# Pooling data loaded into two operand tiles of the input projection, within the projection's last block

## The chip, the cores and the metric

One core of a Trainium2 chip runs the whole program. The metric is the device time in microseconds of one execution. Matrix products run on TensorE (PE); VectorE (DVE), ScalarE (ACT) and GpSimd (POOL) do elementwise work; DMA transfers are issued from the queues of SyncE (SP) and ACT.

## The reference

One decoder block on 1024 tokens of width 1024, in float32: half a SwiGLU FFN, a mixer, half a second SwiGLU FFN, and a final norm. The mixer has one input projection and two branches, attention and pooling, which are merged by gates:

```python
u = rms_norm(h, mix_norm[l])
proj = u @ w_in[l]
q = proj[..., o:o + ATTN_WIDTH]...      # and k, v
pz = proj[..., o:o + POOL_WIDTH]
gates = jax.nn.sigmoid(proj[..., o:o + N_BRANCHES * D_MODEL].reshape(B, S, N_BRANCHES, D_MODEL))
y_attn = dilated_mixture_attention(q, k, v) @ w_branch_attn[l]
y_pool = multiscale_pool(pz, pool_w[l], pool_scale[l]) @ w_branch_pool[l]
merged = gates[:, :, 0] * y_attn + gates[:, :, 1] * y_pool
h = h + merged @ w_out[l]
```

`multiscale_pool` takes, in four groups of 128 channels, trailing means over 2, 4, 8 and 16 tokens minus the token, and multiplies each group by its own 128 x 128 matrix. Its result, 512 channels for each token, is what the change is about.

## The kernel before

Float32 accuracy is had by splitting each operand into a rounded part and a rest (`hi` and `lo`) and taking three products (`three`, L119): hi with hi, hi with lo, lo with hi.

**The input projection** (L1292 on) works in 19 blocks (`MIX`, L110): nine for queries, keys and values, two for the pooling input, eight for the gates; the last is gate block 7. A block is multiplied in seven products instead of eight, in the order 1, 6, 2, 7, 5, 4, 3 (`ORDER`, L317), each of twelve matmuls (`Sevens.product`, L309). Each product has its own left operand made of the normed input, a pair of tiles hi and lo of 128 x 4 x 512 floats (1 MB each) that stays in SBUF for the whole projection: product 1 reads `b11`, 2 reads `b21`, 3 `b22`, and 4 to 7 read `t4`, `t1`, `t2`, `t3` (L363). In traces, where digits are left out of names, `xhi_b_mix` is any of the three b tiles, `xhi_t_mix` any of the four t tiles. So the last block reads `b11` for the last time in its first product, `b21` in its third, `b22` in its seventh.

The loop over k (L1297) runs over all products of all blocks. At a given k it also issues the transfers of that place in the order: results of a finished block go to DRAM (`gate` L1007, `late_w` L1130, `pool` L1093 with `pool_dram` g for pooling group g), and the attention's first data are brought in: `first_ring` at k = n - 12, `load_values(0)` and `load_branch(0)` at k = n - 4, with n the number of products.

**The attention** (L1714 on) works in rounds q, each on two tiles of queries. TensorE does in a round: the scores (L1479), the transposes `tp` of the round before (L1526), up to eight matmuls `yp` of the pooling branch (`branch`, L1604 to L1620), and the values `o` of the round before that (L1559). ACT does the exponents (L1506) that the transposes need. The matmuls `yp` fill the waiting time of TensorE: for each output block d they take weights `wab` and, in the order k = 2, 3, 0, 1, the four pooling groups `y_pool[k]`, three matmuls for each group.

Queries and keys of the next 8 tiles come as a ring: eight loads `qk_in` (L1143, L1144), four for the queries and four for the keys, from `load_ring`; then ACT (L1152) and POOL (L1153) split them in place, `split_ring` n = 0, 1 for the first four loads in one round and n = 2, 3 for the other four in the next. In rounds 0 to 3 the kernel works on ring 0 and splits the second pair (ring 1) in rounds 2 and 3.

**Order.** Both stretches are under `tc.manual_schedule()`: the instructions of each engine stand in the order in which the code is written, and each queue issues its transfers in that order, one waiting for the next. Semaphores are put in by the framework; it gives each transfer one of eight in turn, and a transfer waits until the one that had its semaphore before has landed. SBUF places are handed on tile by tile: a tile in a place that was used before waits for the last reader of the tile that lay there (`reuse_waits="tile"`, L160).

**The four pooling tiles** lie in pools of their own, opened behind the projection (L1337) in the place where `b21` and `b11` lay. Their loads (L1602, named `pool_in<-pool`) are the first of the attention's transfers:

```python
    y_pool = [left_b.enter_context(sbuf(f"pool{g}")).tile([P, 2, S], F32R, name=f"pool_in{g}") for g in range(4)]
...
        for g in (2, 3, 0, 1):
            load_pool(g)
        load_ring(uses[1], ring_tile)
        load_branch(1)
```

Of the kernel before, what the change touches and what calls it, by code (L numbers as in the profile page):

```python
# [10 lines left out]
F32 = mybir.dt.float32  # L11
F32R = mybir.dt.float32r
# [4 lines left out]
P = 128  # L17
S = 1024
# [108 lines left out]
def tile_block(  # L127
# [28 lines left out]
    nc = tc.nc  # L156
    ve, ac, gp, pe = nc.vector, nc.scalar, nc.gpsimd, nc.tensor

    def sbuf(name, side="left", bufs=1):
        return tc.tile_pool(name=name, bufs=bufs, side=side, reuse_waits="tile")  # L160
# [13 lines left out]
    def row(name):  # L174
        return keep.tile([P, 1024], F32, tag="raw", bufs=RAW_BUFS, name=name)
# [109 lines left out]
    def sums_of_x(pool, name, order, **kw):  # L285
        return {
            s: tuple(pool.tile([P, 4, HALF], F32R, name=f"x{part}_{s}_{name}", **kw) for part in ("hi", "lo"))
            for s in order
        }
# [329 lines left out]
    def spilled(name):  # L619
        return [  # L620
            [dram.tile([P, js.stop - js.start, HALF], F32, name=f"gs_{name}{m}_{js.start}") for js in PAIRS]
            for m in range(7)
        ]
# [268 lines left out]
        return pairs  # L892

    sums = spilled("f1")
    mstack, dstack = ExitStack(), ExitStack()
    X_mix = {}

    def down_room(name):
        return dstack.enter_context(sbuf(f"down_{name}"))

    def room1():
        scope.close()
        X_mix.update(sums_of_x(mstack.enter_context(sbuf("xa")), "mix", ("b21", "b11")))
        return down_room("f1")

    def load_residual():
# [25 lines left out]
    pool_dram = [dram.tile([P, 2, S], F32, name=f"pool{g}") for g in range(4)]  # L932
# [164 lines left out]
    def load_pool_w():  # L1097
        pool_w_in.append(fm.tile([P, 2, HALF], F32R, tag="y", bufs=2, name="pool_w"))
        nc.sync.dma_start(pool_w_in[0].bitcast(F32), late_w[0])
# [3 lines left out]
    def load_table(g):  # L1103
        tables[g] = keep.tile([P, 2, HALF], F32, tag="gain", bufs=1, name=f"table{g}_in")
        nc.sync.dma_start(tables[g], table_dram[g])
# [30 lines left out]
    def load_ring(u, tile):  # L1136

        ring[u] = []
        for a in range(2):
            y, hi = tile(F32, f"qk{u}_{a}_in"), tile(F32R, f"qk{u}_{a}_hi")  # L1140
            for n in range(2):
                r = n * HD + 16
                nc.sync.dma_start(y[r:r + 48], qk_dram[u][a, n, 16:])  # L1143
                nc.sync.dma_start(y[r - 16:r].rearrange("r (t c) -> r t c", t=2),  # L1144
                                  rot_dram[u][1][:, a, n].rearrange("t r c -> r t c"))
            ring[u].append((hi, y.bitcast(F32R), y))

    def split_ring(u, n):

        hi, lo, y = ring[u][n // 2]  # L1150
        c = (LOWS, HIGHS)[n % 2]
        ac.activation(hi[:, c], y[:, c], AF.Copy)  # L1152
        gp.tensor_tensor(lo[:, c], y[:, c], hi[:, c].bitcast(F32), op=OP.subtract)  # L1153

    def first_ring():
        load_ring(0, lambda dt, n: keep.tile([P, S], dt, tag="h", bufs=NT, name=n))
        yield 4
        for n in range(4):
            split_ring(0, n)
            yield 1  # L1160
# [4 lines left out]
    def row_part(name):  # L1165
        return keep.tile([P, S], F32R, tag="raw", bufs=RAW_BUFS, name=name)
# [6 lines left out]
            nc.sync.dma_start(v.bitcast(F32), v_dram[u][:, part])  # L1173


    pool_in = {}

    def load_branch(d):
        w, gb = row_part(f"wab{d}"), row(f"gb{d}")
        nc.sync.dma_start(w.rearrange("p (q c) -> p q c", q=2).bitcast(F32), late_w[1 + d][:, :, 256:768])  # L1180
        nc.sync.dma_start(gb, gate_dram[d][:, 1])
        pool_in[d] = (w.rearrange("p (q c) -> p q c", q=2), gb)
# [5 lines left out]
    items = [(q, m) for q in range(len(MIX)) for m in ORDER if q >= AHEAD or m not in (1, 2)]  # L1188
# [103 lines left out]
    with tc.manual_schedule():  # L1292
        entry.run(high_mix, after_mix)

        later, results = [], {}
        load_table(0)
        for k in range(len(items) + 4):  # L1297
            if k - 1 in results and items[k - 1][1] == 1:
                mixes[items[k - 1][0]].out(1, results.pop(k - 1))
            mix_operand(k + 2)  # L1300
            if k - 2 in range(len(items)):
                mixes[items[k - 2][0]].activate()
            if k < len(items):
                q, m = items[k]
                results[k] = mixes[q].quad.run(m)
                if m == 7 and 0 < q <= len(LATE):
                    later.append([k + 1, split_late(q - 1)])
            if k - 1 in results:
                q, m = items[k - 1]
                mixes[q].out(m, results.pop(k - 1))  # L1310
                if m == 3:
                    later.append([k, mixes[q].finish()])
            for job in list(later):
                if job[0] <= k:
                    wait = next(job[1], 0)
                    job[0] = k + wait
                    if not wait:
                        later.remove(job)
            if k == 7 * 6:
                load_pool_w()  # L1320
            if k == 7 * 12:
                tables.clear()
                mask = keep.tile([P, 384], F32, tag="gain", bufs=1, name="mask")
                nc.sync.dma_start(mask, c_mask)
            if k == len(items) - 12:
                later.append([k, first_ring()])
            if k == len(items) - 4:
                load_values(0, row_part)
                load_branch(0)
    assert not later  # L1330
    mstack.close()
    mix_stack.close()
# [1 line left out]


    left_b = ExitStack()
    y_pool = [left_b.enter_context(sbuf(f"pool{g}")).tile([P, 2, S], F32R, name=f"pool_in{g}") for g in range(4)]  # L1337
    sums_o = left_b.enter_context(sbuf("sums_o"))
    ep = left_b.enter_context(sbuf("weights"))
    a2 = left_b.enter_context(sbuf("a2", bufs=2))  # L1340
# [257 lines left out]
    by_pool = [dram.tile([P, S], F32, name=f"by_pool{d}") for d in range(KT)]  # L1598
    stores = []

    def load_pool(g):
        nc.sync.dma_start(y_pool[g].bitcast(F32), pool_dram[g])  # L1602

    def branch(n):  # L1604

        d, half = divmod(n, 2)
# [105 lines left out]

    first = first_w_o()
    with tc.manual_schedule():  # L1714
        for g in (2, 3, 0, 1):
            load_pool(g)
        load_ring(uses[1], ring_tile)
        load_branch(1)
        factors = [make_factors(hp, eng) for hp, eng in enumerate((gp, ve))]
        combines = [[combine(hp, half, adds, lower) for half in range(2)]  # L1720
                    for hp, (adds, lower) in enumerate((((gp, gp), gp), ((gp, ve), ve)))]
        splits = {}
        for q in range(N // 2):
            send()
            scores(2 * q)
            scores(2 * q + 1)
            if q > 0:
                trans_p(q - 1)
                splits[q - 1] = split_p(q - 1)
                next(fill, None)  # L1730
                if q % 4 != 3:
                    next(fill, None)
            if q > 1:
                values(q - 2)
            if q > 2:
                gather(2 * q - 6)
                gather(2 * q - 5)
            masked(2 * q)
            masked(2 * q + 1)
            u, i = divmod(q, NT // 2)  # L1740
            if 0 < u < len(uses) - 1 and i == 0:
                load_ring(uses[u + 1], ring_tile)
            if q > 0:
                advance(splits[q - 1], 2)
            if i > 1 and u + 1 < len(uses):
                split_ring(uses[u + 1], 2 * i - 4)
                split_ring(uses[u + 1], 2 * i - 3)
            end_branches()
            exponents(2 * q)
            exponents(2 * q + 1)  # L1750
            house(2 * q)
            house(2 * q + 1)
        send()
        right_b.close()
        load_ya(3)
        load_merge(0)
        load_merge(1)
        open_w_o()
        q = N // 2
        trans_p(q - 1)  # L1760
        splits[q - 1] = split_p(q - 1)
        advance(factors[1])
        next(fill, None)
        values(q - 2)
        gather(2 * q - 6)
        gather(2 * q - 5)
        advance(splits[q - 1], 2)
        advance(factors[1], 2)
        next(fill, None)
        end_branches()  # L1770
        values(q - 1)
        for s in range(2 * q - 4, 2 * q):
            gather(s)
        for n in range(8):
            advance(combines[1][n // 4])
            if n != 3:
                next(fill, None)
            end_branches()
            send()
            if n == 3:  # L1780
                load_merge(2)
        for k in (3, 4):
            load_merge(k)
    assert next(fill, None) is None
    left_b.close()


    x2, m1 = ExitStack(), ExitStack()
# [342 lines left out]
```

## Time and profile before

| | |
|---|---|
| time, median of 3 runs | 1957.8 us (1957.8 to 1959.87) |
| profiled execution | span 1955.6 us, from its first to its last instruction; no other time of it is given |
| mean granted TensorE clock | 0.994 |
| input projection's last block and the attention's first rounds | about 1038 to 1083 us of the span |
| `pool_in<-pool` | 4 loads of 1024 KB, issued 1052.7 to 1056.6 us |

In the rows of a timeline the first number is the start in us, the second the time taken, then engine, line, operation, output <- inputs, shapes, and how many instructions the row merges; a bracket gives the idle time of the engine before it and what ended it. SPq and ACTq are the DMA queues of those engines; there the time is that of the issue, and the landing comes later. In a row of groups the numbers behind the bar are busy us, mean ns of one, and idle time before with what ended most of it. In a row of waits they are us in total, times, and the longest.

### The profile page before, as it was taken

To read this page: it belongs to the slowest core of one execution; us is meant where nothing else is said; L and a number is where in the kernel's file an instruction comes from. 1 tells how busy PE (TensorE), PEld (TensorE's weight loads), DVE (VectorE), ACT (ScalarE), POOL (GpSimd) and SP (SyncE) were. 2 spreads that over 40 slices of the span, in tenths; PEclk is the share of its full clock that TensorE was granted. 3 is DMA by queue.
4 is the path that set the end of the run, shared out by engine and by line. 5 is a ranking of instruction groups with operands and counts; after the bars stand their busy time and mean duration, and the time that the engine had idled before them with its cause. 6 is when DMAs were issued, how large, how long until landed. Compare 5 with 4: busy or idle time off the path is not lost. (4 is left out here: it accounts for less than half of the span.)

```text
span 1955.6 us, 25018 instructions
## 1 busy us (share of the span) xinstructions
PE 1914.1 (98%) x8938; PEld 1579.7 (81%) x8938; DVE 1343.5 (69%) x2012; ACT 759.4 (39%) x1361; POOL 741.1 (38%) x557
## 2 busy tenths in 40 slices
PE   9999999999999999999998999999999999999997
PEld 7788888888888887888876878887788888878885
DVE  7776556557686876568774886887665556577766
ACT  6333333334344533334344662253333333333343
POOL 5333333332222444445454365543333333322231
PEclk9999999999999999999998999999999999999999
DMA  4155223336465546765658887643523223454653
GB/s 185 44 194 169 85 86 117 121 124 208 156 246 201 167 120 230 232 220 185 232 218 289 241 241 261 253 161 96 190 102 135 82 87 120 139 204 135 212 195 142
DMA packets 147005, 333.57 MB, mean 171 GB/s; under 512 B 20160, under 2 KB 40896, under 8 KB 145344
## 3 DMA queue, kind: packets, MB, share of 16 engines
q1 hardware_dynamic: 138096, 308.00, 45.9%
q10 hardware_dynamic: 8784, 23.96, 3.5%
q8 instruction: 71, 1.16, 0.2%
q14 instruction: 54, 0.44, 0.1%
HBM read 229.61 MB, written 102.30 MB: 170 GB/s over the span
## 5 line engine op out<-in xcount | busy, mean ns | idle before, releaser
L706 PE MATMUL d_f<-bhi_f,alo_f 128*128 128x512 f32 x616 | 240.8, 391 | 2.4 <-POOL alo_f L668 2.2
L706 PE MATMUL d_f<-bhi_f,ahi_f 128*128 128x512 f32 x616 | 240.9, 391 | 0.2 <-ACT ahi_f L664 0.2
L706 PE MATMUL d_f<-blo_f,ahi_f 128*128 128x512 f32 x616 | 240.0, 390 | 0.0
L668 POOL TENSOR_TENSOR alo_f<-g_f,ahi_f 128x512 fp32r<-128x512 f32 x70 | 99.2, 1434 | 298.5 <-ACT ahi_f L664 289.8
L314 PE MATMUL u_mixm<-xhi_t_mix,wc_mixm 128*128 128x512 f32 x608 | 196.0, 393 | 2.7 <-POOL wc_mixm L306 2.3
L314 PE MATMUL u_mixm<-xhi_b_mix,wc_mixm 128*128 128x512 f32 x456 | 149.3, 393 | 2.0 <-DVE y_m L982 2.0
L706 PEld LDWEIGHTS d_f<-bhi_f,alo_f 128*128 128x128 f32 x616 | 115.7, 188 | 29.0 <-POOL alo_f L668 4.0
L314 PEld LDWEIGHTS u_mixm<-xhi_t_mix,wc_mixm 128*128 128x128 f32 x608 | 113.8, 188 | 29.0 <-POOL wc_mixm L306 4.9
L706 PEld LDWEIGHTS d_f<-bhi_f,ahi_f 128*128 128x128 f32 x616 | 115.8, 188 | 24.1 <-ACT ahi_f L664 0.6
L706 PEld LDWEIGHTS d_f<-blo_f,ahi_f 128*128 128x128 f32 x616 | 115.8, 188 | 23.8
L314 PE MATMUL u_mixm<-xlo_t_mix,wc_mixm 128*128 128x512 f32 x304 | 118.6, 390 | 0.0
L306 POOL TENSOR_TENSOR wc_mixm<-s_mixm,wc_mixm 128x512 fp32r<-128x512 f32 x52 | 75.8, 1459 | 99.7 <-ACT wc_mixm L303 84.0
L314 PEld LDWEIGHTS u_mixm<-xhi_b_mix,wc_mixm 128*128 128x128 f32 x456 | 85.7, 188 | 20.7 <-ACT late_hi L1125 2.8
L303 ACT ACTIVATE wc_mixm<-s_mixm 128x512 fp32r<-128x512 f32 x76 | 47.6, 629 | 122.8 <-DVE s_mixm L347 52.1
L314 PE MATMUL u_mixm<-xlo_b_mix,wc_mixm 128*128 128x512 f32 x228 | 88.9, 390 | 0.0
L664 ACT ACTIVATE ahi_f<-g_f 128x1024 fp32r<-128x1024 f32 x84 | 81.8, 974 | 2.0 <-DMA g_f<-gs_f 2.0
L306 POOL TENSOR_TENSOR wc_mixm<-raw,wc_mixm 128x512 fp32r<-128x512 f32 x40 | 60.4, 1515 | 44.9 <-ACT wc_mixm L303 42.0
L664 ACT ACTIVATE bhi_f<-s_f2w 128x512 fp32r<-128x512 f32 x55 | 32.8, 627 | 97.1 <-DVE s_f2w L684 86.8
L1854 PE MATMUL wo<-w_o,o_hi 128*128 128x512 f32 x224 | 69.3, 391 | 0.0
L314 PEld LDWEIGHTS u_mixm<-xlo_t_mix,wc_mixm 128*128 128x128 f32 x304 | 57.2, 188 | 11.7 <-DVE xlo_t_mix L385 0.2
L664 ACT ACTIVATE bhi_f<-s_f1w 128x512 fp32r<-128x512 f32 x55 | 32.9, 630 | 85.1 <-DVE s_f1w L684 80.2
L1616 PE MATMUL yp<-pool_in,wab 128*128 128x512 f32 x192 | 55.7, 426 | 4.2 <-DMA pool_in<-pool 4.2
(1300 smaller groups left out, 5099.8 us busy)
## 6 DMA issues: line engine op xcount, KB each, us to landing
g_f<-gs_f SPq DMA_DIRECT2D x70, 512.0 KB, 4.5
gs_f<-y_f SPq DMA_DIRECT2D x88, 256.0 KB, 2.3
raw<-in_w2a_dram SPq DMA_DIRECT2D x35, 512.0 KB, 4.1
raw<-in_w2b_dram SPq DMA_DIRECT2D x35, 512.0 KB, 4.0
gs_f<-gb_f SPq DMA_DIRECT2D x46, 256.0 KB, 2.3
raw<-in_w1a_dram SPq DMA_DIRECT2D x22, 512.0 KB, 4.6
raw<-in_w3a_dram SPq DMA_DIRECT2D x22, 512.0 KB, 6.3
raw<-in_w1b_dram SPq DMA_DIRECT2D x22, 512.0 KB, 4.5
```

Of the source, the lines that this page charges most:

```text
L303: ac.activation(w[:, 0], src, AF.Copy)
L306: eng.tensor_tensor(w[:, 1], src, w[:, 0].bitcast(F32), op=OP.subtract)
L314: pe.matmul(p, a, b, start=(start and k == 0 and q == 0), stop=(k == 3 and q == 2), skip_group_check=not start)
L664: ac.activation(hi[:, c], src, AF.Copy)
L668: eng.tensor_tensor(lo[:, d], src[:, o], hi[:, d].bitcast(F32), op=OP.subtract)
L706: pe.matmul(self.banks[m][t], l, r, start=(first and q == 0), stop=(last and q == 2))
L1616: pe.matmul(p, a, b, start=(j == 0), stop=(j == 11))
L1854: pe.matmul(banks[m][t], l, r, start=(st == 0 and j == 0 and q == 0), stop=(st == 1 and j == 1 and q == 2))
```

## The change

The tiles of `b11` and `b21` get a stack of pools of their own (`xstack`), which stays open until the attention's end; the other operands are closed with the projection as before. The four pooling tiles have no pools of their own any more: `load_pool` writes pooling group g into one of the four tiles (hi or lo of `b11` or `b21`), seen as 128 x 2 x 1024. Groups 2 and 3 are loaded at k = n - 5, groups 0 and 1 at k = n - 3, inside the projection's loop; the four loads at the head of the attention are gone. In the SP queue of the built program the loads of groups 2 and 3 now stand behind ring 0 and ahead of the last two `late_w` stores, and those of groups 0 and 1 where the first two pooling loads stood before, behind `wab` and `gb` of `load_branch(0)`. The order of all other instructions on every engine stays.

```diff
-    mstack, dstack = ExitStack(), ExitStack()
+    xstack, mstack, dstack = ExitStack(), ExitStack(), ExitStack()
...
-        X_mix.update(sums_of_x(mstack.enter_context(sbuf("xa")), "mix", ("b21", "b11")))
+        X_mix.update(sums_of_x(xstack.enter_context(sbuf("xa")), "mix", ("b21", "b11")))
...
-    pool_in = {}
+    pool_in, y_pool = {}, {}
+
+    def load_pool(g, x, part):
+        y_pool[g] = X_mix[x][part].rearrange("p (q k) c -> p q (k c)", q=2)
+        nc.sync.dma_start(y_pool[g].bitcast(F32), pool_dram[g])
...
+            if k == len(items) - 5:
+                load_pool(2, "b11", 0)
+                load_pool(3, "b11", 1)
             if k == len(items) - 4:
                 load_values(0, row_part)
                 load_branch(0)
+            if k == len(items) - 3:
+                load_pool(0, "b21", 0)
+                load_pool(1, "b21", 1)
...
-    y_pool = [left_b.enter_context(sbuf(f"pool{g}")).tile([P, 2, S], F32R, name=f"pool_in{g}") for g in range(4)]
...
-    def load_pool(g):
-        nc.sync.dma_start(y_pool[g].bitcast(F32), pool_dram[g])
-
...
-        for g in (2, 3, 0, 1):
-            load_pool(g)
         load_ring(uses[1], ring_tile)
...
     left_b.close()
+    xstack.close()
```

## The prediction

> **What bounds the kernel now.** I read the page first, then TensorE's own timeline at the end of the input projection, then the issues of the SP queue there, then the DMA share in short windows.
>
> ```profile
> span 1955.6 us, 25018 instructions
> PE 1914.1 (98%) x8938; PEld 1579.7 (81%) x8938; DVE 1343.5 (69%) x2012; ACT 759.4 (39%) x1361; POOL 741.1 (38%) x557
> L1616 PE MATMUL yp<-pool_in,wab 128*128 128x512 f32 x192 | 55.7, 426 | 4.2 <-DMA pool_in<-pool 4.2
> ```
>
> TensorE is busy for 98% of the span, so what can be won is its idle time and the time in which it runs slowly. The pooling branch `yp` idles 4.2 us, all of it for the four loads of `pool_in` (128 x 2 x 1024 floats, 1.05 MB each). Its mean matmul is 426 ns against 0.39 us for a matmul of the projection (quoted further down), so some of them also ran slowly. Where:
>
> ```profile
> 1056.94 0.33 PE L1479 MATMUL s<-qk_hi,qk_hi 64*128 64x128 f32 x2
> 1061.18 0.71 PE L1526 MATMUL tp<-ident,e 128*128 128x128 f32 x2 [1.39 <-ACT e L1506]
> 1062.74 1.52 PE L1616 MATMUL yp<-pool_in,wab 128*128 128x512 f32 x3
> 1065.63 1.65 PE L1616 MATMUL yp<-pool_in,wab 128*128 128x512 f32 x3 [1.36 <-DMA pool_in<-pool]
> 1069.78 1.22 PE L1616 MATMUL yp<-pool_in,wab 128*128 128x512 f32 x2 [2.50 <-DMA pool_in<-pool]
> 1074.49 1.87 PE L1616 MATMUL yp<-pool_in,wab 128*128 128x512 f32 x7 [0.38 <-DMA pool_in<-pool]
> 1077.36 0.39 PE L1479 MATMUL s<-qk_hi,qk_hi 64*128 64x256 f32 x2
> ...
> 1088.05 0.33 PE L1479 MATMUL s<-qk_hi,qk_hi 64*128 64x128 f32 x2
> 1089.56 2.07 PE L1616 MATMUL yp<-pool_in,wab 128*128 128x512 f32 x8
> 1091.47 0.28 PE L1559 MATMUL o<-ehi,v_in 128*128 128x256 f32 x1
> 1092.99 0.33 PE L1479 MATMUL s<-qk_hi,qk_hi 64*128 64x128 f32 x2
> ```
>
> The loads land one by one: 2 before 1062.74, 3 at 1065.6, 0 at 1069.8, 1 at 1074.5. Undisturbed, eight `yp` take 1091.47 - 1089.56 = 1.91 us and one round (scores, transposes, eight `yp`, values) 1092.99 - 1088.05 = 4.94. From 1062.74 these make 6.85; the kernel needs 14.62 to reach 1077.36. So 7.77 us are lost here, by waits and by the clock:
>
> ```profile
> 1059.53:1062.94 3.41, 1.76 (x12) 0.94 (x9) 1.12 (x7) 3.22 (x10) 0.00 (x0) 0.99 1.01 399
> 1062.94:1073.18 10.24, 6.38 (x25) 3.88 (x24) 2.18 (x9) 2.55 (x9) 0.00 (x0) 0.50 1.02 387
> 1131.21:1134.62 3.41, 3.41 (x11) 2.58 (x10) 3.37 (x13) 3.41 (x12) 2.52 (x2) 0.51 1.04 329
> ```
>
> (Stretch, length, busy us of PE, PEld, DVE, ACT, POOL, granted clock, DMA share, GB/s.) After a stretch of 3.41 us with 1.76 busy the clock is half for 10.24 us, which is three such stretches. At 1131, where TensorE had work all through, one stretch at half clock was all.
>
> **The change part by part.** Nothing is computed differently. In the built program's SP queue two issues move: loads 2 and 3 go from behind `wab` and `gb` to ahead of the last `late_w` stores; loads 0 and 1 stay behind `gb`. The destinations are now the operand tiles b11 and b21 themselves.
>
> ```profile
> 1036.27 0.30 SPq L1144 DMA_DIRECT2D qk_in<-rot  x1
> 1043.44 4.04 SPq L1130 DMA_DIRECT2D late_w<-raw  x2
> 1051.31 0.61 SPq L1180 DMA_DIRECT2D wab<-late_w  x1
> 1052.65 4.22 SPq L1602 DMA_DIRECT2D pool_in<-pool  x4
> 1057.94 0.33 SPq L1143 DMA_DIRECT2D qk_in<-qk  x1
> 1068.46 0.30 SPq L1144 DMA_DIRECT2D qk_in<-rot  x1
> 1072.33 0.30 SPq L1144 DMA_DIRECT2D qk_in<-rot  x1
> ```
>
> *The new wait.* Load 2 must wait for the last block's first product, the last reader of b11. In TensorE's timeline the product behind it, on t2, begins at 1040.53:
>
> ```profile
> 1040.53 0.39 PE L314 MATMUL u_mixm<-xhi_t_mix,wc_mixm 128*128 128x512 f32 x1
> ```
>
> So load 2 can go near 1041. SP has nothing to issue between 1036.6 and 1043.44, so the wait holds up nobody.
>
> *The transfer.* The DMA engines in that time:
>
> ```profile
> 1042.00:1048.00 6.00, 6.00 (x28) 4.97 (x27) 3.36 (x3) 4.32 (x9) 6.00 (x5) 1.00 0.23 91
> 1048.00:1050.00 2.00, 2.00 (x10) 1.67 (x9) 0.69 (x1) 0.40 (x1) 2.00 (x2) 1.00 1.01 401
> ```
>
> At 401 GB/s 2.1 MB take 5.2 us. From about 1042 (a microsecond after issue, my estimate) to 1048 the engines are idle for 0.77 of 6 us, 4.6. So 0.6 us of it pushes back what follows, for from 1048 on the engines are full.
>
> *Whether that hurts.* `wab` had landed at 1057.9, when the ring issue that waits for it went out (1057.94 above); 1058.5 is still ahead of the first `yp` at 1062.74, and 4.8 us of cover were there. Load 0 takes the place of load 2, which landed after 9.3 us at 1062.0: now 1062.6, needed six `yp` into the round, not before 1064. Load 1 takes that of load 3: 1065.6 becomes 1066.2, needed 1062.74 + 1.91 + scores and transposes (1089.56 - 1088.05 = 1.51) + one `yp` = 1066.4. All four waits of `yp` go.
>
> ```profile
> L1602 SPq DMA_DIRECT2D pool_in<-pool x4: 319/376/498, 1052.7 to 1056.6; - x4
> DMA to landing us min/median/max: 9.3/13.4/17.9
> ```
>
> *What stays.* The gap of 1.39 before 1061.18 is ACT's and isn't touched, so the half clock from 1062.94 stays for one stretch, which is then full: half of 3.41, or 1.7, is kept. TensorE's own gain is 7.77 - 1.7 = 6.1.
> The Trainium skill ("TensorE: Matmul & The Clock Gate", section "HAM oscillation — how this bites in real kernels") warns only of idle gaps over some 3.4 us. By it 1.39 would not slow the array and the gain would be 7.8; the row above, where 1.76 busy of 3.41 was enough, speaks against it.
>
> *What is late next.* The attention's second pair of rings (`qk_in`, eight loads in two halves). ACT splits them in its order, ahead of the exponents that TensorE's transposes need:
>
> ```profile
> 1076.52 1.15 ACT L1152 ACTIVATE qk_hi<-qk_in 128x512 fp32r<-128x512 f32 x2 [1.97 <-DMA qk_in<-rot]
> 1080.67 1.14 ACT L1152 ACTIVATE qk_hi<-qk_in 128x512 fp32r<-128x512 f32 x2
> ...
> SPq L1144 <- DMA gate<-y_m: 9.2, 2, 6.2
> L1007 ACTq DMA_DIRECT2D gate<-y_m x2: 326/416/506, 1058.4 to 1058.8; - x2
> DMA to landing us min/median/max: 10.0/11.8/13.5
> ...
> L1144 SPq DMA_DIRECT2D qk_in<-rot x2: 303/303/303, 1072.3 to 1074.5; - x2
> DMA to landing us min/median/max: 3.1/3.8/4.5
> ```
>
> Every DMA of this program takes the next of eight semaphores and first waits for the DMA that had it before; so the rings' issues at 1068.46 and 1072.33 waited for ACT's two gate stores, issued at 1058.4 and 1058.8, landed 10.0 and 13.5 us later. In the changed program the first ring half waits for `v`, `wab` and `gb`, is out by 1060 (`gb` follows `wab` on the queue) and lands some 2 us behind load 1 (as at 1076.5 behind 1074.5): 1068.5, when ACT gets there. The second half still waits for both gate stores, whose issue doesn't move. Bounds for the second store: 1069.5, if it has the engines to itself once SP's queue is dry near 1069, and 1072.3 as now. I take 1071.7, nearer the row, since the first ring half keeps SP's queue full. The last issue follows at 1072.1 and lands 3.1 later (last row above, up to 4.5): 1075.2. ACT then splits at 1075.2 what it splits at 1080.67 now: **5.4 us** earlier, less than TensorE's 6.1. Bounds of that term: 1072.3 + 0.4 + 4.5 = 1077.2, a gain of 3.5; with 1069.5, TensorE's 6.1.
>
> After that every step follows the one before. The third pair of rings starts only some 2.5 us earlier, since it is issued behind the second, but has cover:
>
> ```profile
> L1144 SPq DMA_DIRECT2D qk_in<-rot x1: 303/303/303, 1085.7 to 1085.7; - x1
> DMA to landing us min/median/max: 3.7/3.7/3.7
> ...
> 1095.29 1.15 ACT L1152 ACTIVATE qk_hi<-qk_in 128x512 fp32r<-128x512 f32 x2
> ```
>
> It lands at 1089.4 and is used at 1095.3, so 5.9 us of cover against 5.4 - 2.5 = 2.9 of it used.
>
> *Sum.* Span 1955.6 - 5.4 = 1950.2. The profile shows no time of its own execution beside the span; the median of the runs is 1957.8, so 2.2 us lie around it, and the forecast is 1952.4.
>
> **The rivals.**
> *The rings come in time.* The gate stores land by 1070, and TensorE's own 6.1 us (clock half for one stretch) to 7.8 (for none, where the stretches divide the gap otherwise than in this execution) are won: 1951.7 to 1950.0. For it: fewer loads compete with the store. Against: the store shares the engines until the first ring half has landed.
> *Given back later.* In the attention's middle POOL waits for a load of weights:
>
> ```profile
> POOL w_o_in L1371 <- DMA w_o_in<-in_w_o_dram: 6.9, 1, 6.9
> ```
>
> ACT splits that weight behind POOL and ahead of exponents, so TensorE may stop behind it. If loads there run at the engines' rate, they come earlier only by the 2.5 us of the third rings, so about 3 of 5.4 are lost: gain 2.5, 1955.3. Against: the rows from 1088 to 1093 above show no wait for a load.
> *It doesn't do what it says.* Load 2 gets its place only when b21's reader is done, two products of twelve matmuls later (8 take 1.91 us, so 5.7), at 1046.3: at most the 1.7 us up to 1048 are left to use, and so gained: 1956.1. Against: the two tiles have wait and place of their own.
> *Slower.* Load 2 waits at the head of SP's queue until the whole block is done, when the scores begin at 1056.9, and `late_w`, the gate stores, `v`, `wab` and `gb` stand behind it. With the four pools (4.2 MB), 1.05 for each of the first three and 0.5 for each of the last two these are 8.4 MB, 21 us at 401 GB/s, and 2 for landing: load 1 lands at t + 23 for an issue at t. Against 1074.5 that loses from t = 1051.5 on; at 1056.9 it costs 5.4: 1963.2. Against: b11's reader is the block's first product.
>
> **How the numbers follow.** Chances: forecast 0.50, rings in time 0.20, given back 0.16, not as it says 0.06, slower 0.08. 0.2% (3.9 us) is what a measurement of this kernel tells from no change. Faster by more: the forecast but for its upper end (0.45), the rings in time (0.20) and a part of the third (0.04): 0.69. Slower 0.08, the rest 0.23. The range runs from 1949.5 (7.8 and half a microsecond between runs) to 1956.5, over the third and fourth cases; the forecast's own bounds are 1951.7 to 1954.3.
>
> **What would show it.** Loads 2 and 3 issued near 1041 and landed by 1049; no idle time of `yp` for a load; one stretch at half clock after 1062.9, not three; the scores of 1077.36 near 1071; a wait of ACT's L1152 for `qk_in` of 1 to 2 us near 1075. The forecast is wrong if SP's `late_w` starts after 1044, if `wab` lands after 1062.7, or if TensorE is 5 us ahead at 1085 and not at 1200.

## The result, and the profile after

| | before | changed kernel |
|---|---|---|
| time, median (lowest to highest, runs) | 1958.0 us (1955.9 to 1963.3, 15) | 1954.8 us (1951.4 to 1956.4, 15) |
| ratio of the runs | | 0.9976, 95% interval 0.9969 to 0.9983 |
| profiled execution: time and span | span 1955.6 us | 1953.8 us, span 1951.8 us |

The change makes the kernel faster by 0.24% (0.17 to 0.31), which is 4.7 us (3.3 to 6.1) of 1958; the medians stand 3.2 us apart. 5.4 were forecast, with 3.5 to 6.1 as the bounds of that term.

TensorE's timeline of the changed kernel, from the first scores on. Line numbers behind L1176 are 4 to 9 higher than before in this part, `pool_in` is now called by the tile in which it lies (`xhi_b_mix`, `xlo_b_mix`), and the whole trace runs 0.71 us later from the first scores on (1057.65 for 1056.94). This shift is there before any of the moved loads and is not of the change.

```profile
1057.65 0.33 PE L1488 MATMUL s<-qk_hi,qk_hi 64*128 64x128 f32 x2
...
1061.98 0.71 PE L1535 MATMUL tp<-ident,e 128*128 128x128 f32 x2 [1.47 <-ACT e L1515]
...
1063.68 1.63 PE L1622 MATMUL yp<-xhi_b_mix,wab 128*128 128x512 f32 x3
...
1066.87 0.39 PE L1488 MATMUL s<-qk_hi,qk_hi 64*128 64x256 f32 x2
...
1070.80 0.28 PE L1568 MATMUL o<-ehi,v_in 128*128 128x256 f32 x1
...
1071.95 0.39 PE L1488 MATMUL s<-qk_hi,qk_hi 64*128 64x256 f32 x2
...
1073.49 1.92 PE L1535 MATMUL tp<-ident,e 128*128 128x128 f32 x8 [0.57 <-ACT e L1515]
...
1088.28 0.33 PE L1488 MATMUL s<-qk_hi,qk_hi 64*128 64x128 f32 x2
```

No `yp` waits for a load any more, the scores of 1077.36 come at 1071.95, and those of 1092.99 at 1088.28. Counted from the first scores of the same trace (called t0 from here on), these last ones come at 30.63 us instead of 36.05: 5.42 less. They are the sixth group of scores in the timeline, those of round 6; most expectations below call them "the eighth scores". The expectation of again_after uses the same words for the fourth group: its 25.5 and 20.0 us are 1082.41 - 1056.94 before and 1077.70 - 1057.65 after.

The clock and the DMA engines (stretch, length, busy us of the five engines, granted clock, DMA share, GB/s):

```profile
1059.38:1062.79 3.41, 1.78 (x11) 0.87 (x8) 1.83 (x12) 2.64 (x8) 0.00 (x0) 1.00 0.98 392
1062.79:1066.20 3.41, 3.35 (x10) 2.66 (x11) 1.11 (x2) 2.90 (x12) 0.00 (x0) 0.50 1.03 430
...
1042.70:1048.70 6.00, 6.00 (x28) 4.97 (x27) 3.25 (x3) 4.43 (x9) 6.00 (x5) 1.00 0.96 329
```

One stretch at half clock, where three were. The last row is the time into which loads 2 and 3 went, the same six microseconds that carried 91 GB/s before.

SP's queue, issues only, and the landings of some of them:

```profile
1041.43 0.34 SPq L1180 DMA_DIRECT2D xhi_b_mix<-pool  x1
1041.82 0.43 SPq L1180 DMA_DIRECT2D xlo_b_mix<-pool  x1
1044.14 3.92 SPq L1130 DMA_DIRECT2D late_w<-raw  x2
...
1050.95 0.85 SPq L1184 DMA_DIRECT2D wab<-late_w  x1
1051.90 0.57 SPq L1185 DMA_DIRECT2D gb<-gate  x1
1052.57 0.40 SPq L1180 DMA_DIRECT2D xhi_b_mix<-pool  x1
1056.79 0.32 SPq L1180 DMA_DIRECT2D xlo_b_mix<-pool  x1
...
1062.06 0.30 SPq L1144 DMA_DIRECT2D qk_in<-rot  x1
1068.67 0.31 SPq L1143 DMA_DIRECT2D qk_in<-qk  x1
```

```profile
L1180 SPq DMA_DIRECT2D xlo_b_mix<-pool x1: 431/431/431, 1041.8 to 1041.8; - x1
DMA to landing us min/median/max: 5.1/6.6/8.1
...
L1184 SPq DMA_DIRECT2D wab<-late_w x1: 854/854/854, 1050.9 to 1050.9; - x1
DMA to landing us min/median/max: 9.8/9.8/9.8
...
L1180 SPq DMA_DIRECT2D xlo_b_mix<-pool x1: 320/320/320, 1056.8 to 1056.8; - x1
DMA to landing us min/median/max: 12.2/12.2/12.2
...
L1144 SPq DMA_DIRECT2D qk_in<-rot x1: 302/302/302, 1062.1 to 1062.1; - x1
DMA to landing us min/median/max: 9.6/9.6/9.6
```

The first answer is of loads 2 and 3 together. Load 2 lands at 1046.5 (1041.43 + 5.1), load 3 at 1049.9 (1041.82 + 8.1), `wab` at 1060.75, load 1 at 1069.0, and the last load of the first ring half (issued at 1062.06) at 1071.7. That one ends ACT's wait:

```profile
1068.48 1.08 ACT L1547 ACTIVATE ehi<-tp 128x512 fp32r<-128x512 f32 x2 [1.85 <-PE tp L1535]
1071.80 1.15 ACT L1152 ACTIVATE qk_hi<-qk_in 128x512 fp32r<-128x512 f32 x2 [2.24 <-DMA qk_in<-rot]
...
1075.94 1.14 ACT L1152 ACTIVATE qk_hi<-qk_in 128x512 fp32r<-128x512 f32 x2
```

ACT reached the split of the second rings at 1069.56 and stood for 2.24 us. The second half of these rings, which the prediction took for the late one, was split at 1075.94 without a wait.

### The profile page after: what moved, and what is told of

Its sections match the earlier page's. It is cut to its first block, busy times and chain, and to the rows that moved or that the text cites. A ratio compares the mean times of both kernels' runs of the same rounds, so it can differ in the third digit from the quotient of the medians.

```text
span 1951.8 us, 25018 instructions
## 1 busy us (share of the span) xinstructions
PE 1912.8 (98%) x8938; PEld 1577.6 (81%) x8938; DVE 1342.7 (69%) x2012; ACT 759.3 (39%) x1361; POOL 740.2 (38%) x557
## 4 chain that ended last, share of the span: by engine, by line
PE 35%; DMA 5%; DVE 3%; issue 3%; POOL 2%; ACT 1%; SPq 1%; POOLq 0%; DVEq 0%; ACTq 0%
PE d_f L706 7%; PE wo L1859 3%; DMA v_in<-v 1%; PE u_mixm L314 1%; PE u_f210a L314 1%; PE u_f29b L314 1%; PE u_f29a L314 1%; PE u_f28b L314 1%; PE u_f28a L314 1%; PE u_f27b L314 1%; PE u_f27a L314 1%; PE u_f26b L314 1%; PE u_f26a L314 1%; PE u_f25b L314 1%; PE u_f25a L314 1%
## 5 line engine op out<-in xcount | busy, mean ns | idle before, releaser
L668 DVE TENSOR_TENSOR blo_f<-raw,bhi_f 128x1024 fp32r<-128x1024 f32 (+1 forms) x24 | 30.0, 1250 | 39.0 <-ACT bhi_f L664 39.0
```

Source lines behind the costliest of these rows:

```text
L668: eng.tensor_tensor(lo[:, d], src[:, o], hi[:, d].bitcast(F32), op=OP.subtract)
```

## The experiments

For each kernel: where ACT's first split of the second rings begins (with its wait for them), where TensorE's first values `o` begin, and where the scores of round 6 begin, all in us behind t0; then the median time and the ratio to the kernel before. The first three columns come from one profiled execution of each kernel. The ratio of after is to the first row; every other ratio is to new runs of the kernel before, taken beside that kernel, with medians of 1958.7 to 1959.3. So the ratios compare better than the medians. The last three kernels hold an edit beyond the change.

| kernel | split (wait) | values | round 6 | median, us (runs) | ratio, 95% interval |
|---|---|---|---|---|---|
| before | 19.58 (1.97) | 19.25 | 36.05 | 1958.0 (15) | |
| again_before | 19.01 (1.90) | 19.08 | 35.47 | 1957.6 (11) | 0.9992, 0.9983 to 1.0001 |
| after | 14.15 (2.24) | 13.15 | 30.63 | 1954.8 (15) | 0.9976, 0.9969 to 0.9983 |
| again_after | 14.78 (1.95) | 14.51 | 31.27 | 1952.3 (5) | 0.9966, 0.9954 to 0.9979 |
| old_order | 15.93 (4.04) | 15.50 | 32.39 | 1955.0 (9) | 0.9976, 0.9966 to 0.9986 |
| gate_late | 12.86 (1.70) | 12.36 | 29.37 | 1953.3 (6) | 0.9968, 0.9956 to 0.9979 |
| fill | 14.42 (3.60) | 13.73 | 30.89 | 1952.1 (5) | 0.9967, 0.9954 to 0.9979 |
| gb_behind_ring | 11.69 (none) | 12.80 | 33.51 | 1956.5 (11) | 0.9993, 0.9984 to 1.0002 |
| all_early | 19.63 (none) | 20.75 | 36.88 | 1959.0 (11) | 1.0002, 0.9993 to 1.0011 |
| gate_late_before | 17.37 (1.10) | 17.43 | 33.85 | 1957.5 (11) | 0.9986, 0.9977 to 0.9995 |
| two_tiny | 14.66 (2.46) | 14.53 | 31.13 | 1954.1 (11) | 0.9976, 0.9967 to 0.9985 |
| w_o_early | 13.78 (1.76) | 13.02 | 30.25 | 1949.7 (5) | 0.9961, 0.9947 to 0.9974 |
| gate_late_w_o_early | 13.25 (2.35) | 12.46 | 29.72 | 1947.6 (5) | 0.9948, 0.9933 to 0.9964 |
| gate_late_gb_mid_w_o_early | 13.23 (2.34) | 11.89 | 29.57 | 1947.3 (5) | 0.9947, 0.9932 to 0.9961 |

One pattern runs through the table. In all twelve executions in which ACT waited for the ring, round 6 comes 16.34 to 16.51 us behind that split, while the values lie anywhere from 11.89 to 19.25. As long as ACT waits for the first ring half, what the change is worth is what it takes from the landing of that half; where TensorE stands before that does not count. It was the same before the change (16.47 and 16.46), where three waits of `yp` stood in plain view (1.36, 2.50 and 0.38 us; in again_before two, 3.53 and 0.19). The expectations below call this the ring theory; the TensorE theory is that TensorE's own idle time and clock set the time.

### The two kernels again

> The kernel before, unchanged, for a second profile and for the spread between executions. If the difference of 0.71 us that the two profiles already show when the scores begin (1056.94 before, 1057.65 after) is chance, this profile has its scores begin anywhere from 1056 to 1059. Theory 1 (four waits for loads and a half clock for three stretches belong to the order of the loads) expects idle time of 3.5 to 5 us at the matmuls yp for loads, and the loads landing one by one between 1062 and 1075. Rival (the profile of before caught an unlucky execution) expects clearly less than 3 us.

> The changed kernel, unchanged, for a second profile. Theory 1 expects no wait of yp for a load, and ACT's first split of the second pair of rings waiting 1.5 to 3 us for its loads, with the eighth scores 20.0 us behind the first (25.5 before). Rival (the wait for the rings was chance) expects that wait to be gone and the eighth scores 18.5 us behind the first. Time: ratio 0.997 to 0.999 to before.

The kernel before, run against itself, gives 0.9992, so 0.1% is what such a ratio can be off by. Its second profile waits 3.72 us at `yp` for loads, has its first scores at 1057.46 and three stretches at half clock, so what the first one shows is not chance. The changed kernel gives 0.9966, 6.7 us of 1958 (4.1 to 9.0); with the first set's 4.7 this brackets the local gain, 35.76 - 30.95 = 4.8 us as the mean of the two pairs of profiles. In the second profile load 1 was not in time: one `yp` waited 0.42 us for it, and the clock was half for 6.83 us instead of 3.41. The fourth group of scores came 20.67 us behind t0, against 20.0 expected and 18.5 by the rival. Round 6 still came 16.49 us behind the split.

### The loads in the old place of the code, but into the new tiles

```diff
-            if k == len(items) - 5:
-                load_pool(2, "b11", 0)
-                load_pool(3, "b11", 1)
...
     with tc.manual_schedule():
+        load_pool(2, "b11", 0)
+        load_pool(3, "b11", 1)
+        load_pool(0, "b21", 0)
+        load_pool(1, "b21", 1)
         load_ring(uses[1], ring_tile)
```

> The changed kernel with all four loads at the head of the attention again, in the order 2, 3, 0, 1, but still into the tiles of b11 and b21. Theory 1 (only the queue's order matters) expects the time of before: ratio 0.9990 to 1.0010, waits of yp for loads of 3.5 to 5 us. Rival 2 (the place or the stack of the pools matters) expects the time of the changed kernel, 0.9976.

In the built program load 2 was issued at 1041.49, ahead of `late_w`, all the same, and loads 3, 0 and 1 behind `gb`, from 1053.26 on. So this is not the order of before but half of the change: one load of 1.05 MB moved instead of two. It lies in between: split at 15.93 against 19.0 to 19.6 and 14.2 to 14.8, one wait of `yp` left (2.37 us, for load 1). All four loads have the new tiles here, so the tiles by themselves don't give the whole gain; that they give none of it this run can't show, as one load moved with them. What speaks against them is the queue of the kernel before: its four pooling loads waited 2.5 us for `v` to land and, for a last reader, not at all (0.2 us in again_before), so the old place held up nothing. In time this kernel can't be told from the changed one.

### The last gate store behind the second rings

```diff
         def store(self):
             yield 3
-            queue = nc.sync if self.q < len(MIX) - 1 else nc.scalar
+            if self.q < len(MIX) - 1:
+                self.put()
+
+        def put(self):
             for a in range(2):
-                queue.dma_start(gate_dram[self.g][:, a], self.y[a])
+                nc.sync.dma_start(gate_dram[self.g][:, a], self.y[a])
...
         load_ring(uses[1], ring_tile)
+        mixes[-1].put()
```

On the changed kernel (gate_late), and on the kernel before (gate_late_before):

> The changed kernel with the last gate store taken from ACT's queue and put behind the second pair of rings on SP's queue. Theory 3 (what is left is ACT: 0.96 us of issuing the store ahead of the exponents, and the rings' loads sharing the engines with the store and waiting for its semaphores) expects the first transposes 0.9 us earlier, the gap of 1.47 us at 0.5, perhaps no stretch at half clock (1.7 us), ACT's wait for the rings below 1 us, and 2 to 3.5 us less than the changed kernel: ratio 0.9960 to 0.9967 to before. Rival 4 (the rings are late because the engines are full, with or without the store) expects 0.5 us at most: ratio 0.9973 to 0.9978.

> The kernel before with the last gate store moved from ACT's queue to SP's, behind the second rings. Ring theory: the last load of the first ring half no longer waits for the store's semaphore until 1068.5, and 1.05 MB less share the engines; the first half can land right behind pooling load 1, so ACT's split comes up to 2.0 us earlier (its whole wait for the ring), eighth scores at 33.5 to 35 us behind the first instead of 35.5 to 36.1, time 1 to 2 us less. TensorE theory: the four yp still wait for loads one by one until 17 us behind the first scores, and the time stays.

Both gain locally: 1.3 to 1.9 us on the changed kernel (29.37 against 30.63 and 31.27), 1.6 to 2.2 on the kernel before (33.85 against 35.47 and 36.05). With 1.05 MB of the store out of the way, the last pooling load on the old order landed early enough for one of its waits to go, and the ring came 1.6 to 2.2 us earlier. The time hardly shows it. On the kernel before the ratio is 0.9986 with an interval below 1, but within the 0.1% that the same kernel is off by against itself; on the changed kernel it is 0.9968, between the 0.9976 and 0.9966 of that kernel. There the gain is given back at the weight load some 65 us behind t0, as shown with w_o_early. Two finer expectations did not come true: ACT still waited 1.70 us for the ring, and one stretch at half clock stayed.

### The clock, and the place of gb

fill puts ten matmuls into TensorE's gap ahead of the first transposes; gb_behind_ring moves 0.5 MB from ahead of the ring to behind it.

```diff
+        for _ in range(10 if q == 0 else 0):
+            pe.matmul(banks[0][:, :P], ones, ones, start=True, stop=True)
```

```diff
     def load_branch(d):
-        nc.sync.dma_start(gb, gate_dram[d][:, 1])
...
+        if d:
+            load_gate(d)
...
         load_ring(uses[1], ring_tile)
+        load_gate(0)
```

> The changed kernel with ten matmuls of ones ahead of the attention's first transposes, into the bank that these write next, so that TensorE has work in its 1.4 us gap there. In six executions so far the eighth scores came 16.46 to 16.51 us after ACT's first split of the second rings, wherever TensorE stood before (its values, two rounds earlier, lay between 12.4 and 19.3 us behind the first scores). Ring theory (the landing of the first half of the second rings alone sets what follows): the half clock behind the gap goes, TensorE is up to 1.7 us earlier, but ACT's split stays 14.2 to 14.8 us behind the first scores, its wait for the ring grows from 2 to 3 or 4 us, the eighth scores stay at 30.6 to 31.3, and the time is that of the changed kernel within 0.1%. TensorE theory (its own idle time and clock set the time): the eighth scores come 1.7 us earlier, at 28.9 to 29.6, and the time falls by 1.7 us.

> The changed kernel with the load gb of the first output block (0.5 MB) moved from ahead of pooling load 0 to behind the second rings. Ring theory, with the DMA engines full: 0.52 MB at 400 GB/s are 1.3 us less ahead of the first ring half, so ACT's first split comes at 12.9 to 13.5 us behind the first scores and the eighth scores at 29.3 to 30.0, 1.3 us less in time. TensorE theory: pooling loads 0 and 1 were there in time already, so nothing changes, eighth scores at 30.6 to 31.3. A third way: gb comes late for VectorE's product of the first pooling block, which stands ahead of its later work; then VectorE shows a wait for gb and the gain is lost.

fill, a window (columns as above), then TensorE's and ACT's timeline:

```profile
1061.00:1066.00 5.00, 4.92 (x34) 4.06 (x34) 1.74 (x6) 4.84 (x17) 0.00 (x0) 1.00 1.00 414
```

```profile
1070.08 0.97 PE L1624 MATMUL yp<-xlo_b_mix,wab 128*128 128x512 f32 x3 [1.64 <-DMA xlo_b_mix<-pool]
...
1072.49 1.15 ACT L1152 ACTIVATE qk_hi<-qk_in 128x512 fp32r<-128x512 f32 x2 [3.60 <-DMA qk_in<-rot]
```

The clock stays full, TensorE reaches its second scores at 8.13 us behind t0 instead of 9.22, and all of it ends in two longer waits: 1.64 for load 1, 3.60 for the ring. Split, round 6 and time are those of the changed kernel. That is what the ring theory expected; TensorE's own clock is worth nothing here.

gb_behind_ring, ACT's, VectorE's and TensorE's timeline:

```profile
1070.15 1.15 ACT L1152 ACTIVATE qk_hi<-qk_in 128x512 fp32r<-128x512 f32 x2
...
1076.65 0.69 DVE L1640 TENSOR_TENSOR gb<-yp,gb 128x512 f32<-128x512 f32 x1 [5.55 <-DMA gb<-gate]
...
1077.48 1.09 PE L1539 MATMUL tp<-ident,e 128*128 128x128 f32 x4 [3.50 <-DVE gb L1640]
```

The first ring half was there before ACT was (issued 1060.74, landed 9.2 later, 11.5 behind t0), earlier than the 1.3 us of its bytes allow. But `gb` was issued at 1070.87 only, held by the rings' waits for the gate stores in front of it, landed 5.7 later, and VectorE and then TensorE stood for it: the third way of the expectation. In time the gain of the change can't be seen any more (0.9993), though round 6, at 33.51, still came 2.0 to 2.5 us earlier than before the change.

### All four pooling loads ahead of late_w

```diff
                 load_pool(3, "b11", 1)
+                load_pool(0, "b21", 0)
+                load_pool(1, "b21", 1)
...
-            if k == len(items) - 3:
-                load_pool(0, "b21", 0)
-                load_pool(1, "b21", 1)
```

> The changed kernel with pooling loads 0 and 1 moved right behind 2 and 3, ahead of late_w, the gate stores, v, wab and gb; they wait at the head of SP's queue for the last reader of b21, 5.7 us behind that of b11, until about 1047. Ring theory: the DMA engines have loads 2 and 3 to carry until then, so no time of theirs is lost, the same bytes stand ahead of the first ring half, and the eighth scores stay at 30.6 to 31.3 us behind the first, though wab now lands 2.1 MB later and the first yp waits some 2 to 4 us for it. TensorE theory: these 2 to 4 us, and a second stretch at half clock (1.7), are lost: eighth scores at 33 to 36. Head-of-queue theory (the wait stops everything behind it): SP issues late_w some 3 us later than in the changed kernel, all that follows comes 3 us later, eighth scores near 34.

SP's queue and TensorE's timeline of this kernel, then who the queue waited for (us, times, longest):

```profile
1047.35 0.32 SPq L1180 DMA_DIRECT2D xhi_b_mix<-pool  x1
...
1050.66 7.16 SPq L1173 DMA_DIRECT2D v_in<-v  x2
1059.37 0.61 SPq L1184 DMA_DIRECT2D wab<-late_w  x1
...
1070.66 1.65 PE L1621 MATMUL yp<-xhi_b_mix,wab 128*128 128x512 f32 x3 [6.02 <-DMA wab<-late_w]
```

```profile
SPq L1180 <- PE u_mixm L314: 8.5, 2, 4.5
SPq L1173 <- DMA xlo_b_mix<-pool: 6.3, 1, 6.3
```

The ring theory's expectation failed: round 6 came at 36.88, later than either of the others had it (33 to 36, and near 34), and the time is that of before. Load 0 held the queue for 4.5 us until b21's reader was done, and that moved `late_w` from 1044.14 to 1048.24. The larger part came behind it: the second load of `v` had the semaphore of load 3 or 1, waited 6.3 us for its landing, and `wab` behind it was issued at 1059.37 instead of 1050.95 and landed 11.3 later. TensorE stood 6.02 us for `wab`. The wait at the head of the queue, one of the rivals of the prediction, is real; the change escapes it because loads 2 and 3 wait for the block's first product and loads 0 and 1 stand behind `gb`.

### Bytes, or the turn of the semaphores

The change also moves the turn of the eight semaphores: before it the fourth and the sixth ring load waited for the gate stores, since then the fifth and the seventh, so the first half is free of them. two_tiny turns it further back and leaves the rest.

```diff
+        for g in (2, 3):
+            tiny = att_small.tile([1, 64], F32, name=f"tiny{g}")
+            nc.sync.dma_start(tiny, pool_dram[g][:1, 0, :64])
         load_ring(uses[1], ring_tile)
```

> The changed kernel with two loads of 256 bytes (one partition, never read) where pooling loads 2 and 3 stood before the change, ahead of the second rings. Nothing else moves, but the turn of the eight semaphores does: now the third load of the first ring half waits for the first of ACT's gate stores, and the fifth ring load for the second; before the change these were the fourth and the sixth, in the changed kernel the fifth and the seventh. Backlog theory (the bytes ahead of the first ring half on the DMA engines set when it lands): ACT's first split stays at 14.2 to 15.5 us behind the first scores, the eighth scores at 30.7 to 32.0, and the time within 0.1% of the changed kernel's. Semaphore theory (the change gained because it freed the first ring half of the gate store): the third and fourth ring loads are issued when the store has landed, 11 us behind the first scores, and land up to 8 us later as before the change; ACT's split comes at 17 to 19, the eighth scores at 33.5 to 35.5, the gain of the change mostly gone.

SP's queue and ACT's timeline, then the landing of the load of 1068.32:

```profile
1062.66 0.32 SPq L1144 DMA_DIRECT2D qk_in<-rot  x1
1067.98 0.30 SPq L1143 DMA_DIRECT2D qk_in<-qk  x1
1068.32 0.42 SPq L1144 DMA_DIRECT2D qk_in<-rot  x1
...
1073.03 1.15 ACT L1152 ACTIVATE qk_hi<-qk_in 128x512 fp32r<-128x512 f32 x2 [2.46 <-DMA qk_in<-rot]
```

```profile
L1144 SPq DMA_DIRECT2D qk_in<-rot x1: 425/425/425, 1068.3 to 1068.3; - x1
...
DMA to landing us min/median/max: 4.6/4.6/4.6
```

The last load of the first half went out 9.95 us behind t0 instead of 4.41, and landed 4.6 us later instead of 9.6: within 0.5 us of the same place, 14.5 against 14.0. When it is issued hardly matters within 5.5 us; it lands when what stands ahead of it has gone. So the turn of the semaphores is not what the change gains by, and what is left is the transfers that it takes out of the queue's backlog.
The Trainium skill ("DMA: Bandwidth & Descriptors", section "Queues, rings and completion order") says that each DMA engine takes one queue's descriptors in order and changes between queues packet by packet; two_tiny agrees with the first half of this. The local gain of both kernels with the ACT store moved away (1.3 to 2.2 us) agrees with engines that two queues share; no run here shows the packets.

### The second place, and a faster kernel

```diff
-            for _ in range(3):
+            for _ in range(5 - 2 * st):
                 yield
...
-        if N - 28 <= s < N - 13:
+        if N - 30 <= s < N - 13:
             advance(first)
```

w_o_early issues the first two loads of `w_o_in` one round earlier and uses them where it did; the next kernel adds gate_late's edit, the last also puts `gb` between the two halves of the ring.

> The changed kernel with the first two loads of w_o_in issued one round (two steps) earlier, ahead of wab, gb, v and the statistics there; its use stays where it was. In the profiles so far POOL waits 6 to 8 us for it near 1120 and TensorE, behind ACT, 1.2 to 3.2 us, with one or two stretches at half clock behind that wait. If this load is the second place at which the DMA queue sets the end: TensorE's wait there goes, a half-clock stretch (1.7 us) perhaps too, and the time falls by 1.5 to 3.5 us below the changed kernel. If the engines are full there (share 0.97) and only the order changes: something behind it (v, the rings) comes late by as much, and the time stays within 0.1%.

> Both: the last gate store behind the second rings on SP's queue, and w_o_in one round earlier. With the gate store moved alone the eighth scores came at 29.4 instead of 30.6 to 31.3 us behind the first, but w_o_in landed no earlier (64.7 us behind the first scores in both) and took the gain back. If that is so, here the gain of the ring (1.3 to 1.9 us) stays in addition to that of w_o_in: 1.3 to 1.9 us below the run with w_o_in alone. If the end is set by something else behind it, the two runs are alike.

> As the last one, and the load gb of the first output block stands between the two halves of the second rings instead of ahead of pooling load 0; there no semaphore of a gate store holds it. Ring theory: 0.5 MB less ahead of the first ring half, ACT's first split 1.3 us earlier, at 11.2 to 11.9 us behind the first scores, no wait of ACT for it, eighth scores at 27.8 to 28.6, provided gb lands by 13 us, when VectorE needs it; else VectorE shows a wait for gb and the gain shrinks by it. Time up to 1 us below the last run.

POOL's and TensorE's waits there, first in the changed kernel, then in gate_late:

```profile
1122.35 2.50 POOL L1380 TENSOR_TENSOR w_o_in<-w_o_in,w_o_in 128x512 f32<-128x512 f32 x2 [6.97 <-DMA w_o_in<-in_w_o_dram]
...
1125.48 0.71 PE L1535 MATMUL tp<-ident,e 128*128 128x128 f32 x2 [1.97 <-ACT e L1515]
```

```profile
1123.85 2.49 POOL L1383 TENSOR_TENSOR w_o_in<-w_o_in,w_o_in 128x512 f32<-128x512 f32 x2 [8.27 <-DMA w_o_in<-in_w_o_dram]
...
1126.96 2.05 PE L1538 MATMUL tp<-ident,e 128*128 128x128 f32 x6 [3.24 <-ACT e L1518]
```

Behind t0 the weight is used at 64.70 us in the one and 64.74 in the other, though gate_late's round 6 is 1.3 us earlier: the 1.3 us come back as a longer wait (3.24 for 1.97). In w_o_early and the two kernels with it this wait is gone, and so is the half-clock stretch behind it. Window of the changed kernel, then of w_o_early:

```profile
1121.00:1131.00 10.00, 7.76 (x41) 6.00 (x41) 5.57 (x19) 7.19 (x24) 7.34 (x6) 0.83 0.94 271
```

```profile
1121.00:1131.00 10.00, 10.00 (x75) 8.52 (x74) 9.16 (x37) 8.24 (x26) 4.17 (x4) 1.00 1.01 276
```

Measured from t0, the scores that the changed kernel starts at 1131.67 come 4.9 us earlier in w_o_early, 5.4 and 5.6 in the other two. The last kernel runs in 1947.3 us (0.9947, 0.9932 to 0.9961): its slowest run, 1949.0, lies below the changed kernel's fastest, 1951.4, so it beats both. What gate_late's edit adds on w_o_early (1949.7 to 1947.6) is as large as expected, but the intervals overlap. Moving `gb` between the halves added nothing: the split, expected at 11.2 to 11.9 without a wait of ACT, stays at 13.2 with one of 2.34 us, and VectorE now waits 3.64 us for `gb`.

## Why the prediction was right or wrong

*The issue and the place.* Right: loads 2 and 3 went out at 1041.43 and 1041.82, and `late_w` started when it did before (1044.14 with the shift of 0.71, against 1043.44). Load 3 landed at 1049.9, 1049.2 in the time of before, just behind the 1049 that was named.

*The transfer.* This is the term that was mis-sized: "0.6 us of it pushes back what follows". `wab` landed at 1057.9 before (1051.31 + 6.6, the row below) and at 1060.75 after, 60.0 in the time of before: 2.1 us later.

```profile
L1180 SPq DMA_DIRECT2D wab<-late_w x1: 609/609/609, 1051.3 to 1051.3; - x1
...
DMA to landing us min/median/max: 6.6/6.6/6.6
```

I had let the two loads use all the idle time of the engines at 401 GB/s. In the six microseconds the engines were as good as busy (0.96) but carried 329 GB/s instead of 91, which is 1.43 MB of the 2.10; the remaining 0.67 MB at 401 GB/s are 1.7 us of the 2.1. In the second pair of profiles it was 326 instead of 161 GB/s, so 0.99 MB fitted in and 1.11 were left, 2.8 us, and `wab` landed 2.9 us later. The row of idle time was read rightly; the rate at which two transfers fill it was not in that row.

*Whether that hurts.* The prediction speaks of four waits of `yp`; its rows show three, as load 2 was there in time. They went in the first profile, but by little: load 1 landed at 1069.0 (68.3 in the time of before) instead of 1066.2, and in four other executions with these loads in this order it was waited for by 0.28 to 1.64 us (gate_late_w_o_early 0.28, again_after 0.42, two_tiny 1.05, fill 1.64). None of this shows in round 6, as ACT's wait for the ring lay behind.

*The clock.* One stretch at half clock after a stretch with 1.78 of 3.41 busy, as forecast, and two in the second profile; in fill, with the gap closed, there was none. A gap much shorter than 1.47 us was followed by half clock too. In gate_late it was 0.48:

```profile
1062.43 0.71 PE L1538 MATMUL tp<-ident,e 128*128 128x128 f32 x2 [0.48 <-ACT e L1518]
```

There TensorE was busy for 2.65 of the 3.41 us from 1060.39 on, and the next 3.41 us ran at 0.51. Where the border lies between that and fill's 4.92 of 5.00 is not shown. In the section that the prediction names ("HAM oscillation — how this bites in real kernels" of "TensorE: Matmul & The Clock Gate"), the Trainium skill ties the slowing to idle gaps over about 3.4 us; these rows speak against it. The 1.7 us that I booked for the clock were worth nothing either way: the gain in TensorE's own time (6.1 forecast; 19.25 - 13.15 = 6.1 measured, 4.6 in the second pair) is not what reaches the end.

*What is late next.* That the rings set what remains was right, and so was the size: the second split was to come at 75.2 and came at 1075.94, 75.2 in the time of before. The half was wrong. I had the first half land at 1068.5, "when ACT gets there", and the second held back by the gate stores until 1075.2. In fact the first half, pushed back like everything in the queue, landed at 71.0, 2.5 us later than forecast, and the second split follows the first by 4.14 us in any case. The gate stores did hold the second half's issues (the one at 1068.67 waited until the first store had landed, at 1059.15 + 9.5), but it landed at 1074.3, in time. So it is luck that 75.2 came out: I had the first half 2.5 us too early, and took the second, in fact there at 73.6 in the time of before, for the one that ACT waits for. The step that failed here is which half ACT waits for.

*The rivals.* The rings in time: no, ACT waited 1.95 and 2.24 us. Given back later: not by a longer wait. POOL's wait for `w_o_in` stayed as it was (6.88 and 6.97 us in the first pair, 6.24 and 6.30 in the second; TensorE's behind it 1.85 and 1.97, 1.25 and 1.31), the load having moved forward with everything else. The clock behind this wait differs, though: three of these four profiles have a stretch at half clock there and again_before has none. So TensorE's first `wo`, near 1200, comes 5.2 us earlier in the first pair (139.22 for 144.46 behind t0) and only 2.8 in the second (139.09 for 141.87). And this wait is where the next microsecond is lost, as gate_late showed. Slower by a wait at the head of SP's queue: not in the change, but all_early gave all of the gain back by that way and what hangs on it.

*The size in time.* 5.4 locally in the first pair of profiles and 4.2 in the second; 4.7 (3.3 to 6.1) and 6.7 (4.1 to 9.0) by the ratios. The forecast is inside both intervals. The two medians of the first set stand only 3.2 us apart, just under the forecast's own bounds.

## What to carry to other kernels

When an engine's waits for loads stand out, look for the last landing that the next stage needs, and count back from it: if the DMA engines are full between here and there, moving one load gains what that landing gains, and the waits in view are only where the time is spent. For a load moved into idle DMA time, take the rate that transfers had just after the queue was empty, not that of a full queue, and push everything behind it back by the rest. And a wait that is removed is soon followed by the next queue at the same engines: here moving the weight load, used some 65 us behind t0, took another 4.9 us off the timeline of the profiles, as much as the change itself, though the ratios show only 1 to 3 us of it (0.9961 against 0.9976 and 0.9966).

## What the runs showed of the hardware

- With the engines full, a load issued 5.5 us later on the same queue landed within 0.5 us of the same time (9.6 and 4.6 us after issue). Its time to landing here told of the queue ahead of it, not of the load.
- The first six microseconds of a refilled queue carried 329 and 326 GB/s, where the full queue carried 401. From 1042.00 to 1044.00, just behind the issues at 1041.43 and 1041.82, it was 197 GB/s with 0.75 of the engines' time.
- The bytes ahead of a transfer are not all that counts. The first ring half landed 11.5 us behind t0 in gb_behind_ring, where `gb` and the later ring loads were held back, and at 13.2 in the last kernel, where they were issued right behind it and no more bytes stood ahead of it. From 1064 to 1067 the engines were full in both (1.02 and 1.01 of their time) but carried 416 GB/s in the one and 217 in the other. Why is not shown; the share of time in which the engines were busy was no measure of what they moved.
- Half clock for one stretch of 3.41 us came near 774 us, where nothing differs between the kernels, in four of the fourteen profiles (gate_late, gb_behind_ring, two_tiny, w_o_early) and not in the others. In full use it costs 1.7 us (half of 3.41). Over runs of one kernel the mean clock goes with the time: among the runs of the kernel before beside two_tiny, the fastest, 1953.8 us, had 0.997 and the slowest, 1960.9 us, 0.992.
